# The group norm's inverse square root: one third-order step and one Newton step in place of three Newton steps

## The chip, the cores and the metric

The kernel runs on one core of a Trainium2 chip. The metric is the device time of one execution in microseconds (us). Three runs of the kernel before took 1077.81, 1078.03 and 1082.76 us, so the median is 1078.03 us. One more execution, the profiled one, is the source of every row below. The engines are called PE (TensorE matmuls), PEld (its weight loads), DVE (VectorE), ACT (ScalarE), POOL (GpSimd) and SP (SyncE, whose queue issues most transfers).

## What is computed

The reference is one step of a two-layer decoder trunk on 256 prompt tokens and 8 x 8 sample tokens (320 columns together). Layer 0 mixes tokens with a chunked gMLP, layer 1 with a Mamba-2 scan; each mixer is followed by a squared-ReLU MLP. All products are float32. The change touches the end of the Mamba-2 mixer, where the 2048 channels are cut into 8 groups of 256 and every group is divided by its own root mean square, for every token:

```python
y = y.reshape(bsz, l, D_INNER).astype(h.dtype) * jax.nn.silu(z)
yg = rms_norm(y.reshape(bsz, l, SSM_GROUPS, D_INNER // SSM_GROUPS), norm_g.reshape(SSM_GROUPS, -1))
out = yg.reshape(bsz, l, D_INNER) @ w_out
```

`rms_norm` multiplies with `rsqrt(mean(x * x) + EPS)`, where EPS is 1e-6, and with a gain.

## The kernel before, in words

**Layout.** Channels lie on the 128 partitions and the 320 tokens along the free dimension. Weights stream from HBM as tiles of 128 x 1024 (`raw`). `split` (line 133) makes two halves of each: ACT rounds it to `whi` (line 136), DVE subtracts to get `wlo` (line 137). `mm3` (line 305) then issues three matmuls of 320 columns per 128 x 128 block (lines 307 to 309), so that the sum has float32 precision.

**The Mamba stage.** Layer 1's mixer runs over the 8 groups `g_`. For each group, `convs` (line 804) projects six tiles (`in_tile`, 24 matmuls each), and `conv` (line 634) sums four shifted products on ACT and DVE (`co`, lines 646 and 649). `group_loads` (line 668) queues on SP the state and the two broadcast rows of decays (`bc`, line 673, and `ea`). `ssd` (line 677) is a generator, and the loop at line 865 advances the generator of the group before between the conv tiles of the current group, so two groups overlap. Its pieces in order: decay factors (lines 679 to 689, with `bc` computed by ACT at 687 and 688), transposes (693 to 729), state products (733 to 745), the output products (line 757) with `Y` on DVE (768) and POOL (769), then the group norm (773 to 780), then the state update (784 to 802).

**The group norm.** ACT squares `Y` (line 774) and DVE adds the two halves into `ta` (line 776). `mean_rstd` (line 222) lets PE take the mean over the partitions as three one-column products (`mean_mm`, line 210): token t of the block then sits on partition t, and the whole statistic is a tile of 128 x 3. On that tile DVE computes the negative inverse root: line 230 adds EPS, and `neg_rsqrt` (line 194) makes a first guess from the bits of the number (line 195) and refines it by three Newton steps of three instructions (lines 197 to 199). All of these stand in the trace with the tile name `nv`. `bcast` (line 201) then lets PE spread the result over the partitions (line 205: three matmuls with the negated identity `nid`, each of which leaves two records in the trace), and DVE scales `Y` into `yst` (line 780). `yst` is read only after the last group, by the output projection. Groups 0 to 6 go this way. Group 7 uses `root` (line 212) instead, with ACT's square root. `neg_rsqrt` is also called three times in layer 0, at line 537 (tile `mv`).

```python
        for _ in range(3):
            dve.tensor_tensor(a, r, r, MUL)
            dve.scalar_tensor_tensor(a, a, 0.5, v, MUL, MUL)
            dve.scalar_tensor_tensor(r, a, 1.5, r, SUB, MUL)
```

**The order of the work.** The program is written as data flow. A planner orders each engine's instructions at build time by walking through its own model of the times (line 1089, `schedule_with_timeline_sim=True`). On the chip, each engine executes its list in that fixed order. Two exceptions are written out by hand in this stage: `issue_after` at line 761 keeps the output products behind one of their own, and at line 796 the state update's. The statistic's matmuls and the broadcast share one PSUM buffer (pool `psn`, `nrm_ps`, line 110), so the mean of a group waits until line 780 of the group before has read the broadcast.

Of the kernel before, what the change touches and what calls it, by code (L numbers as in the profile page):

```python
# [9 lines left out]
I32 = mybir.dt.int32  # L10
AF = mybir.ActivationFunctionType
ALU = mybir.AluOpType
ADD, SUB, MUL, MIN, MAX = ALU.add, ALU.subtract, ALU.mult, ALU.min, ALU.max
# [18 lines left out]
EPS = 1e-6  # L32
# [20 lines left out]
def tile_trunk(ctx: ExitStack, tc: tile.TileContext, io):  # L53
    nc = tc.nc
    pe, act, dve, pool = nc.tensor, nc.scalar, nc.vector, nc.gpsimd
# [12 lines left out]
    def nm(s):  # L68
        uid[0] += 1
        return f"{s}{uid[0]}"  # L70
# [39 lines left out]
    def nrm_ps():  # L110
        return psn.tile([P, 512], F32, tag="nrm", name=nm("nrm"))
# [82 lines left out]
    def neg_rsqrt(r, v, a):  # L194
        dve.tensor_scalar(r.bitcast(I32), v.bitcast(I32), -0.5, 1597463007.0, MUL, ADD)
# [5 lines that stand above are left out]
    def bcast(r):  # L201
        pr = nrm_ps()
        for c in range(3):
            w = P if c < 2 else TS
            pe.matmul(pr[:, c * P : c * P + w], lhsT=r[:, c : c + 1].to_broadcast([P, P]), rhs=nid[:, P - w :], start=True, stop=True, skip_group_check=True)
        return pr[:, :T]

    def mean_mm(ps, q, ones, first, last):
        for c in range(3):
            pe.matmul(ps[:, c : c + 1], lhsT=q[:, OFFS[c] : OFFS[c] + P], rhs=ones[:, 0:1], start=first, stop=last, skip_group_check=True)  # L210

    def root(ps, t):
        s, v, r, a = (t[:, i, :3] for i in range(4))
        act.activation(s, ps[:, :3], AF.Sqrt, bias=eps)
        dve.tensor_scalar(v, ps[:, :3], EPS, None, ADD)
        dve.reciprocal(r, s)
# [3 lines that stand above are left out]
        return r  # L220

    def mean_rstd(q, ones, last=False):
        ps = nrm_ps()
        mean_mm(ps, q, ones, True, True)
        if last:
            t = tp.tile([P, 4, 4], F32, tag="nx", name=nm("nx"))
            return bcast(root(ps, t))
        s = tp.tile([P, 3, 4], F32, tag="nv", name=nm("nv"))
        v, r, a = s[:, 0, :3], s[:, 1, :3], s[:, 2, :3]
        dve.tensor_scalar(v, ps[:, :3], EPS, None, ADD)  # L230
        neg_rsqrt(r, v, a)
        return bcast(r)

    acc = {}
# [20 lines left out]
    def rstd_x(both=False):  # L255
        ps = acc["ps"]
        t = tp.tile([P, 4, 4], F32, tag="nx", name=nm("nx"))
        pr = bcast(root(ps, t))
        o = tp.tile([P, T], F32, tag="rstd", name=nm("rstd"))
        act.copy(o, pr)  # L260
        return (pr, o) if both else o
# [49 lines left out]
    def proj1(srcs, hi, lo, eng=dve):  # L311
        ps = mm_ps()
        n = 8 * len(srcs)
        for kc, src in enumerate(srcs):
            w = wload(src, eng=eng)
            for kk in range(8):
                k = kc * 8 + kk
                mm3(ps, w, kk, hi(k), lo(k), k == 0, k == n - 1)
        return ps
# [14 lines left out]
    def scaled(ps, r):  # L334
        c = tp.tile([P, 10], F32, tag="sc", name=nm("sc"))
        act.copy(c, ps[:, T:G])
        t = scratch()
        dve.tensor_tensor(t, ps[:, :T], r, MUL)
        dve.tensor_tensor(b1(t[:, TP:]), b1(t[:, TP:]), bb(c[:, 1:9]), ADD)
        dve.tensor_scalar(t[:, :TP], t[:, :TP], c[:, 0:1], None, ADD)  # L340
        return t
# [39 lines left out]
    for k in range(KD):  # L381
        sq = scratch()
        act.activation(sq, x[:, k, :], AF.Square)
        if k:
            a = tp.tile([P, T], F32, tag="acc", name=nm("acc"))
# [7 lines left out]
    v = gp.tile([P, 2, DG], F32, name="v")  # L393
# [188 lines left out]
    for m in range(KD):  # L582
        ps = proj1([io["gm_wo"][m, kc] for kc in range(2)], lambda k: uhi[:, k, :], lambda k: ulo[:, k, :])
# [36 lines left out]
    ps = scaled(pss[0], r0)  # L620
# [56 lines left out]
    def ssd(g_, st, bc, ea, B, C, X, Z):  # L677
# [97 lines left out]
        q1 = scratch()  # L775
        dve.tensor_tensor(q1, q0[:, 0], q0[:, 1], ADD)
        pr = mean_rstd(q1, ones_g, g_ == NG - 1)
        for r in range(2):
            m = 2 * g_ + r
# [180 lines left out]
    pr, r = rstd_x(True)  # L960
# [148 lines left out]
```

## Time and profile before

| what | value |
| --- | --- |
| median of three runs | 1078.03 us (1077.81 to 1082.76) |
| the profiled execution | 1075.66 us, span 1073.9 us |
| PE busy | 1030.2 us, 96% of the span |
| PEld busy | 970.8 us, 90% |
| DVE busy | 652.9 us, 61%, 1080 instructions |
| ACT busy | 549.2 us, 51% |
| POOL busy | 299.9 us, 28% |
| HBM | 199.31 MB read, 12.85 MB written |

The span runs from the first to the last instruction; the 1.76 us between it and the execution's time lie around it. Matmuls overlap in the trace, so a record's duration is longer than the step from its start to the next start. Where PE was idle, the timeline prints how long and what ended it. A DVE instruction's record, too, can overlap that of the next one.

### The profile page before, as it was taken

The numbers are of one execution on the slowest core, as the hardware profiler recorded it, in microseconds if no ns is written. First come the engines' busy times: TensorE is split into PE (matmuls) and PEld (weight loads), VectorE is DVE, ScalarE is ACT, GpSimd is POOL, SyncE is SP. The second block draws the span as 40 slices with busy tenths as digits, with TensorE's granted clock in tenths as the row PEclk, the third lists the DMA queues.
The fourth block names the chain that finished last, engine by engine and source line by source line (L and its number), as shares of the span: only waits on it lengthen the run. The fifth ranks groups of instructions, "written<-read, shape, count | busy, mean of one in ns | idle before, by whom it ended". The sixth has DMA issues, their size and how long they took to land.

```text
span 1073.9 us, 19747 instructions
## 1 busy us (share of the span) xinstructions
PE 1030.2 (96%) x7809; PEld 970.8 (90%) x7809; DVE 652.9 (61%) x1080; ACT 549.2 (51%) x1013; POOL 299.9 (28%) x403
## 2 busy tenths in 40 slices
PE   5999999999999999999688999999999999999996
PEld 3778998999999999999688999999999999999995
DVE  4545966437644443446968898898876754444432
ACT  4453343435644433335698777678345555543331
POOL 1200134332433311222123333532217243411001
PEclk9999999999999999999888999999999999999998
DMA  9957985775666667455435656565445544544431
GB/s 366 361 194 237 335 316 166 267 253 195 243 215 216 217 223 271 151 157 172 151 108 171 251 168 222 197 224 205 167 163 158 177 157 140 155 153 144 155 99 50
DMA packets 60877, 213.97 MB, mean 199 GB/s; under 512 B 6560, under 2 KB 12128, under 8 KB 58480
## 3 DMA queue, kind: packets, MB, share of 16 engines
q1 hardware_dynamic: 58544, 200.47, 55.1%
q0 software_dynamic: 1952, 11.98, 3.1%
q8 instruction: 61, 1.00, 0.4%
q10 hardware_dynamic: 288, 0.26, 0.1%
q14 instruction: 32, 0.26, 0.1%
HBM read 199.31 MB, written 12.85 MB: 198 GB/s over the span
## 4 chain that ended last, share of the span: by engine, by line
PE 76%; ACT 7%; DVE 6%; issue 5%; DMA 3%; POOL 2%; SPq 0%; POOLq 0%; ACTq 0%; DVEq 0%
PE mm L307 19%; PE mm L308 19%; PE mm L309 19%; PE adap L165 3%; ACT bc L687 2%; DMA bc<-rowd 2%; DVE wlo L137 2%; DVE co L649 2%; ACT whi L136 1%; PE mm L411 1%; PE mm L412 1%; PE mm L413 1%; PE ax L757 1%; DMA raw<-ada 1%; PE ax L307 1%
## 5 line engine op out<-in xcount | busy, mean ns | idle before, releaser
L137 DVE TENSOR_TENSOR wlo<-raw,whi 128x1024 fp32r<-128x1024 f32 (+1 forms) x243 | 298.1, 1228 | 203.5 <-ACT whi L136 202.6
L136 ACT ACTIVATE whi<-raw 128x1024 fp32r<-128x1024 f32 (+1 forms) x243 | 254.7, 1050 | 252.4 <-PE mm L308 195.0
L307 PE MATMUL mm<-hhi,whi 128*128 128x320 f32 x952 | 300.1, 316 | 1.9 <-ACT ta L356 0.9
L308 PE MATMUL mm<-hlo,whi 128*128 128x320 f32 x952 | 296.8, 313 | 0.1
L309 PE MATMUL mm<-hhi,wlo 128*128 128x320 f32 x952 | 296.9, 313 | 0.0
L307 PEld LDWEIGHTS mm<-hhi,whi 128*128 128x128 f32 x952 | 180.2, 190 | 7.5 <-issue 3.3
L308 PEld LDWEIGHTS mm<-hlo,whi 128*128 128x128 f32 x952 | 180.1, 189 | 1.9 <-DVE hlo L267 1.0
L309 PEld LDWEIGHTS mm<-hhi,wlo 128*128 128x128 f32 x952 | 180.0, 189 | 1.4 <-DVE mv L198 0.4
L307 PE MATMUL mm<-mhi,whi 128*128 128x320 f32 x512 | 158.3, 309 | 0.0
L308 PE MATMUL mm<-mlo,whi 128*128 128x320 f32 x512 | 158.1, 309 | 0.0
L309 PE MATMUL mm<-mhi,wlo 128*128 128x320 f32 x512 | 158.0, 309 | 0.0
L358 POOL TENSOR_TENSOR ta<-ta 128x320 f32<-128x320 f32 x64 | 82.0, 1285 | 140.0 <-ACT ta L356 118.2
L307 PEld LDWEIGHTS mm<-mhi,whi 128*128 128x128 f32 x512 | 96.1, 188 | 1.2 <-issue 0.8
L308 PEld LDWEIGHTS mm<-mlo,whi 128*128 128x128 f32 x512 | 96.1, 188 | 0.0
L309 PEld LDWEIGHTS mm<-mhi,wlo 128*128 128x128 f32 x512 | 96.1, 188 | 0.0
L293 POOL TENSOR_TENSOR x<-x,rs 128x64 f32<-128x64 f32 x28 | 11.2, 399 | 218.5 <-DVE rs L292 218.5
L359 ACT ACTIVATE mhi<-ta 128x320 fp32r<-128x320 f32 x64 | 30.1, 471 | 81.9 <-POOL ta L358 81.6
L360 DVE TENSOR_TENSOR mlo<-ta,mhi 128x320 fp32r<-128x320 f32 x64 | 33.5, 523 | 59.2 <-ACT mhi L359 59.2
L649 DVE SCALAR_TENSOR_TENSOR co<-cb,vec,co 128x344 f32<-128x344 f32 x96 | 54.7, 585 | 6.1 <-ACT co L646 5.9
L165 PE MATMUL adap<-ara,sc 128*32 128x256 f32 x640 | 43.0, 383 | 0.0
L307 PE MATMUL mm<-uhi,whi 128*128 128x320 f32 x128 | 40.0, 315 | 0.0
L308 PE MATMUL mm<-ulo,whi 128*128 128x320 f32 x128 | 40.0, 315 | 0.0
(340 smaller groups left out, 1691.8 us busy)
## 6 DMA issues: line engine op xcount, KB each, us to landing
raw<-mlp_w SPq DMA_DIRECT2D x128, 512.0 KB, 3.6
ara<-ada_w SPq DMA_DIRECT2D x80, 512.0 KB, 6.3
raw<-w_in SPq DMA_DIRECT2D x48, 512.0 KB, 3.7
raw<-ada SPq DMA_DIRECT2D x16, 512.0 KB, 9.9
raw<-gm_wv SPq DMA_DIRECT2D x16, 512.0 KB, 8.7
raw<-gm_wu SPq DMA_DIRECT2D x16, 512.0 KB, 5.8
raw<-gm_wo SPq DMA_DIRECT2D x16, 512.0 KB, 5.3
st<-state SPq DMA_DIRECT2D x8, 1024.0 KB, 5.5
```

The source lines that it names most:

```text
L136: act.activation(hi[:, :n], raw[:, :n], AF.Copy)
L137: eng.tensor_tensor(lo[:, :n], raw[:, :n], hi[:, :n].bitcast(F32), SUB)
L165: pe.matmul(ps[32 * j : 32 * j + 32, :256], lhsT=sc[:, kb + i, :], rhs=rs[i][:, j * 256 : (j + 1) * 256], start=(kb + i == AB - 1), stop=( ...
L293: (dve if m == KD - 1 else pool).tensor_tensor(x[:, m, TP:], x[:, m, TP:], t0, ADD)
L307: pe.matmul(ps[:, :n], lhsT=whi[:, kk, :], rhs=hi, start=first, stop=False)
L308: pe.matmul(ps[:, :n], lhsT=whi[:, kk, :], rhs=lo, start=False, stop=False)
L309: pe.matmul(ps[:, :n], lhsT=wlo[:, kk, :], rhs=hi, start=False, stop=last)
L358: pool.tensor_tensor(s, t, t, MUL)
L359: act.activation(mhi[:, m, :], s, AF.Copy)
L360: dve.tensor_tensor(mlo[:, m, :], s, mhi[:, m, :].bitcast(F32), SUB)
L649: dve.scalar_tensor_tensor(o[:, :CO], cb[:, k : k + CO], wv(k), o[:, :CO], MUL, ADD)
L687: act.activation(bc[:, h, cq[c]], bc[:, h, cq[c]], AF.Relu, bias=nat[:, c, HG * g_ + h : HG * g_ + h + 1], scale=-1.0)
```

## The change

It replaces the call of `neg_rsqrt` in `mean_rstd` by instructions of its own. `v` now holds 64/9 times the mean plus EPS, through the second operation of the instruction that adds EPS. The first guess from the bits is made as before, now from the scaled number. Then one step of third order follows (with x = r·r·v, r becomes r·(x·x − 10/3·x + 5), in four instructions; the factor 3/8 that such a step carries is taken up by the scaling) and one Newton step with the factor 9/64 folded into its constant (three instructions). The result is again the negative inverse root. Before, a call has 1 + 1 + 9 = 11 DVE instructions; after, 1 + 1 + 4 + 3 = 9. Tiles, buffers, matmuls and transfers are unchanged. Group 7 and layer 0 are not touched.

```diff
@@ -227,8 +227,15 @@
             return bcast(root(ps, t))
         s = tp.tile([P, 3, 4], F32, tag="nv", name=nm("nv"))
         v, r, a = s[:, 0, :3], s[:, 1, :3], s[:, 2, :3]
-        dve.tensor_scalar(v, ps[:, :3], EPS, None, ADD)
-        neg_rsqrt(r, v, a)
+        dve.tensor_scalar(v, ps[:, :3], EPS, 64.0 / 9.0, ADD, MUL)
+        dve.tensor_scalar(r.bitcast(I32), v.bitcast(I32), -0.5, 1597463007.0, MUL, ADD)
+        dve.tensor_tensor(a, r, r, MUL)
+        dve.tensor_tensor(a, a, v, MUL)
+        dve.scalar_tensor_tensor(a, a, -10.0 / 3.0, a, ADD, MUL)
+        dve.scalar_tensor_tensor(r, a, 5.0, r, ADD, MUL)
+        dve.tensor_tensor(a, r, r, MUL)
+        dve.scalar_tensor_tensor(a, a, 0.5 * 9.0 / 64.0, v, MUL, MUL)
+        dve.scalar_tensor_tensor(r, a, 1.5, r, SUB, MUL)
         return bcast(r)
```

## Rows read from the trace of the kernel before

**Rows 1.** The page: span, TensorE's line and its granted clock in 40 slices.
```profile
span 1073.9 us, 19747 instructions
...
PE   5999999999999999999688999999999999999996
...
PEclk9999999999999999999888999999999999999998
```

**Rows 2.** Seven stretches, one per group; each ends with clock, DMA share and GB/s.
```profile
core 0: us, PE busy (x) PEld busy (x) DVE busy (x) ACT busy (x) POOL busy (x), PEclk, DMA share, GB/s
...
615.00:645.00 30.00, 28.59 (x273) 27.66 (x274) 29.41 (x58) 22.28 (x49) 11.31 (x22) 1.00 0.53 174
...
737.00:768.00 31.00, 30.02 (x279) 28.54 (x278) 31.00 (x61) 20.84 (x47) 11.71 (x14) 1.00 0.42 146
...
sum 213.00, PE 209.13 PEld 199.69 DVE 188.11 ACT 141.50 POOL 76.45; mean PE 29.88 PEld 28.53 DVE 26.87 ACT 20.21 POOL 10.92
```

**Rows 3.** Tile nv: counts, ns min/median/max, first and last start; who waited for it.
```profile
L198 DVE SCALAR_TENSOR_TENSOR nv<-nv x21: 145/154/169, 591.9 to 774.3; 128x3 f32<-128x3 f32 x21
...
L230 DVE TENSOR_SCALAR nv<-nrm x7: 146/153/154, 587.3 to 768.2; 128x3 f32<-128x3 f32 x7
...
  DVE yst L780: 5.1, 1
```

**Rows 4.** TensorE's waits from 585 to 798 us: us in total, times, longest.
```profile
PE nrm L205 <- DVE nv L199: 2.0, 2, 1.3
PE adap L713 <- DVE Bst L704: 1.3, 2, 1.0
```

**Rows 5.** VectorE's timeline in group 0: start us, us, what.
```profile
586.80 0.57 DVE L649 SCALAR_TENSOR_TENSOR co<-cb,vec,co 128x344 f32<-128x344 f32 x1
587.29 0.15 DVE L230 TENSOR_SCALAR nv<-nrm 128x3 f32<-128x3 f32 x1
587.36 0.47 DVE L704 SCALAR_TENSOR_TENSOR Bst<-adap,cst,Bst 128x256 fp32r<-128x256 f32 x1
```

**Rows 6.** VectorE's timeline in group 6, at the end of its chain.
```profile
773.94 0.16 DVE L199 SCALAR_TENSOR_TENSOR nv<-nv 128x3 f32<-128x3 f32 x1
774.14 0.16 DVE L197 TENSOR_TENSOR nv<-nv 128x3 f32<-128x3 f32 x1
...
774.53 0.16 DVE L199 SCALAR_TENSOR_TENSOR nv<-nv 128x3 f32<-128x3 f32 x1
```

**Rows 7.** VectorE's and TensorE's timelines in group 1 around line 205.
```profile
626.95 0.15 DVE L197 TENSOR_TENSOR nv<-nv 128x3 f32<-128x3 f32 x1
...
627.66 0.16 DVE L199 SCALAR_TENSOR_TENSOR nv<-nv 128x3 f32<-128x3 f32 x1
...
627.88 0.88 PE L205 MATMUL nrm<-nid,nv 128*128 128x128 f32 x6 [1.30 <-DVE nv L199]
```

**Rows 8.** The same two timelines in group 4.
```profile
704.44 0.15 DVE L197 TENSOR_TENSOR nv<-nv 128x3 f32<-128x3 f32 x1
...
705.62 0.15 DVE L199 SCALAR_TENSOR_TENSOR nv<-nv 128x3 f32<-128x3 f32 x1
...
705.91 0.85 PE L205 MATMUL nrm<-nid,nv 128*128 128x128 f32 x6 [0.70 <-DVE nv L199]
```

**Rows 9.** The chain that ended last, 623 to 629 us: start us, us, what.
```profile
624.11 0.07 DVE nv L198
...
625.34 0.07 DVE nv L199
...
626.57 0.33 SPq L147
...
626.99 4.60 DMA bc<-rowd
```

**Rows 10.** VectorE's and TensorE's timelines in group 5 around line 205.
```profile
747.93 0.15 DVE L199 SCALAR_TENSOR_TENSOR nv<-nv 128x3 f32<-128x3 f32 x1
...
748.87 0.88 PE L205 MATMUL nrm<-nid,nv 128*128 128x128 f32 x6
```

## The prediction

> **What bounds the kernel now.** I read the page first. TensorE is busy for 1030.2 of 1073.9 us [rows 1], so whatever shortens the kernel must either take work from TensorE or remove one of its few idle moments. The change takes no matmul away. Its place comes from the rows of tile `nv`: the seven calls start between 587.3 and 768.2 us [rows 3], one per group of the Mamba stage. So the next view is that stage cut by groups. Over 213.0 us TensorE is busy for 209.13, which leaves 3.87 us idle, and VectorE is busy for 188.11, in single stretches almost throughout (29.41 of 30, 31.00 of 31) [rows 2]. The reader should see two things: TensorE sets the pace, but VectorE has little in hand, and it executes its list in order.
>
> The granted clock is below nine tenths only in the 20th to 22nd of 40 slices, 510 to 591 us [rows 1], and is 1.00 in the stretches shown [rows 2]. The planner walks forward in time, so the list up to the first changed instruction at 587.3 us should stay as it is, and those slices with it. I expect nothing from the clock.
>
> The third view is what TensorE waits for there. Its largest cause is the very chain that is shortened: line 205 waits for line 199 twice, 2.0 us together; the other large one, 1.3 us, is line 713 waiting for `Bst` [rows 4], which comes early in a group, before the refinement steps of the same group.
>
> **What the change removes, and its price.** Each call goes from 11 instructions to 9, all on tiles of 128 x 3, so 7 x 2 = 14 of VectorE's 1080 go. Those left are of the kinds already there; the multiplication by 64/9 rides on line 230 as a second operation. An instruction with two operations (line 198, 154 ns) takes as long as line 230 with one (153 ns) [rows 3], so I cost that edit at nothing. If a second operation did cost something, line 198's range (145 to 169 ns) bounds it by 24 ns, or 0.2 us for seven.
>
> The duration of a record isn't its price. In group 0 the record of line 230 lasts 0.15 us, but the next, independent instruction starts 0.07 us after it [rows 5]. That is the price where other work stands in between. In group 6 the last steps stand alone, each needing the one before, and start 0.20 us apart (773.94, 774.14) [rows 6]. So 14 instructions are worth between 14 x 0.07 = 1.0 us and 14 x 0.20 = 2.8 us of VectorE's time.
>
> The Trainium skill (VectorE: DVE Perf Modes, The DRAIN you can't avoid) says that the next vector operation does not start until the pipe of the last one has emptied. By that rule every removed record would give back its whole 0.154 us, 14 x 0.154 = 2.2 us. The trace disagrees for independent neighbours, where 0.07 us pass while the record still runs [rows 5], so the sum doesn't use it.
>
> How much of this is on the path that sets the end? There are two ways in.
>
> First, **TensorE's own waits on the chain**. In group 1 line 205 starts at 627.88 after 1.30 us of idle time, 0.22 us after the start of the ninth refinement instruction (627.66). The seventh started at 626.95, 0.71 us earlier [rows 7]. With seven steps and the same neighbours, the result is ready 0.71 us earlier. In group 4 the seventh starts at 704.44, the ninth at 705.62, 1.18 us later, and the wait is 0.70 [rows 8], so that wait would go. Together 0.71 + 0.70 = 1.4 us, if line 205 keeps its place among TensorE's instructions. It need not: the planner also sees a shorter chain and may put line 205 earlier by about as much, and the waits stay.
>
> Second, **VectorE's queue**. The chain that ended last passes through `nv` not for its result but for its slot: 0.07 us for line 198 and 0.07 for line 199, behind which VectorE's next split lets SP go on, and SP then issues the load of `bc`, which lands 4.60 us after 626.99 [rows 9]. Two slots fewer ahead of that pull SP's load forward by 0.14 us. If all seven groups have this, it is 7 x 0.14 = 1.0 us. No transfer is added, and none is moved past another by the edit itself.
>
> The two overlap, since both end in TensorE being sooner ready. What comes late next is the mean's product and `Bst`, which the edit doesn't touch. In group 6 nothing is gained: VectorE idles for 5.1 us until line 205 comes [rows 3], as the chain ended at 774.53 + 0.16, long before [rows 6]. I take 1.0 us, the value nearest to the slot that the chain of waits itself shows, with 0 and 2.8 us as ends.
>
> The profiled execution took 1075.66 us, 1.76 around its span of 1073.9, and lies 2.4 below the median of the runs, 1078.03. I take the sum off the median: 1078.03 − 1.0 = **1077.0 us**. What a measurement of this kernel can tell from no change is about 0.5%, or 5.4 us: faster means below 1072.6, slower above 1083.4.
>
> **The rivals.**
>
> *Nothing moves.* For it: five of seven groups don't wait on the chain at all; in the closest of them line 205 starts 0.79 us after the last step has ended (747.93 + 0.15 against 748.87) [rows 10]. Line 780's result is read only after the last group. If the planner also moves line 205 ahead by what the chain got shorter, the 2.0 us of waits stay as well. Against it: VectorE's stretches without any idle time [rows 2]. The time: 1078.0.
>
> The Trainium skill (Perfetto Trace Analysis, Identifying the Most-Contended Engine) says to improve the most contended engine first. On this rule, with TensorE at 209.13 of 213 us, the change gives nothing, as in this rival. The two waits on VectorE in rows 4 speak against it, and no row settles it.
>
> *The planner's new order removes other waits as well.* The list after the first changed instruction is planned anew, and the whole idle time of TensorE in the stage is 3.87 us [rows 2]. If all of it went, the time is 1078.0 − 3.9 = 1074.1. To pass 1072.6 it would have to gain outside the stage too, and there is no changed instruction there. For it speaks only that the order is planned; against it, that waits at line 713 hang on other work.
>
> *Line 205 comes too early.* This is the case on the slower side, and one mechanism. In TensorE's list line 205 is an instruction like any other, and while it waits all matmuls behind it wait. The planner places it by modelled times, in which the small steps may weigh more than on the chip; taking two away then moves line 205 further ahead than the real chain gets shorter. It decides from the point at which line 205 is moved by more than the reserve plus what the chain gains, 0.79 + 0.71 = 1.5 us in the closest group. Price: if all seven groups wait as long as the worst one now, 7 x 1.30 = 9.1 us in place of 2.0, so 1078.0 + 7.1 = 1085.1. For it: the two groups that already wait show that the plan runs ahead of the chip. Against it: five groups have a reserve, and the chain does get shorter on the chip.
>
> *The change doesn't do what it says.* That would be a chain that still has 11 instructions, or a result that needs another step. The diff has nine written out, so I give this no chance.
>
> **How the numbers follow.** Forecast (1075.2 to 1077.7): 0.52. Nothing moves: 0.24. New order better: 0.09, of which I put 0.06 below 1072.6, since a replanned list can change more than I can see here. Line 205 too early: 0.15, of which 0.13 lies beyond 1083.4. So faster 0.06, slower 0.13, same 0.81. The range leaves out at most 2 in 10. Its low end is the time without TensorE's idle time in the stage, 1074.1, less another 1.1 for the spread between the profiled execution and the runs. Its high end is 1083.2, where four of the seven groups (4 x 1.30 = 5.2) would newly wait.
>
> **What would show it right or wrong.** Right: tile `nv` shows 14 records fewer, 63 in place of 77; the slots between independent neighbours stay at about 0.07 us; TensorE's wait at line 205 for the chain falls from 2.0 us to about 0.6; its idle time in the stage goes from 3.87 to about 2.9 us; the clock outside slices 20 to 22 stays. Wrong: line 205 waits in more than two groups, or longer in total than 2.0 us (the third rival); the instructions before 587 us stand in another order, or the low-clock slices change, which I excluded; or TensorE gets a wait in the stage that is not in rows 4.

## The result, and the profile of the changed kernel

Seven runs of the changed kernel have a median of **1090.38 us** (1087.90 to 1096.23), seven of the kernel before on the same chip 1080.55 us (1077.5 to 1084.0). The ratio is **1.0104, interval 1.0080 to 1.0129**: the change costs 1%. In the experiment that ran the changed kernel once more it was 1.0110 [1.0083, 1.0136]. The forecast, 1077.0 us, and its range, up to 1083.2, both miss it. The profiled execution of the changed kernel took 1092.18 us, 1.8 around its span. Medians and ratios leave out slow executions, of which there was one (experiment 13: 1312.96 us at a mean granted clock of 0.731).

The page of the changed kernel, with the lines that answer to [rows 1]:

```profile
span 1090.4 us, 19730 instructions
...
PE 1037.7 (95%) x7809; PEld 976.5 (90%) x7809; DVE 653.8 (60%) x1066; ACT 549.2 (50%) x1013; POOL 302.1 (28%) x403
...
PE   5999999999999999999689999899899999999996
...
PEclk9999999999999999999899999899899999999998
```

VectorE has 14 instructions fewer (1066 for 1080), as the diff says. The busy shares are what they were. What is new stands in the last two lines: in the 26th and the 29th slice, 681 to 709 and 763 to 790 us, TensorE is less busy and its granted clock is lower. Before, both slices read 9.

In the changed kernel seven new lines stand behind line 231, so its line numbers are 7 higher from there: 774 is 781, 713 is 720, 307 is 314. Its tile `nv`, in the view that answers to [rows 3]:

```profile
L230 DVE TENSOR_SCALAR nv<-nrm x7: 149/155/161, 589.1 to 776.0; 128x3 f32<-128x3 f32 x7
...
L237 DVE SCALAR_TENSOR_TENSOR nv<-nv x7: 147/155/168, 597.4 to 789.4; 128x3 f32<-128x3 f32 x7
```

There are nine such lines with seven records each, 63 in place of 77. Line 230 now has two operations and takes 155 ns at the median, where it took 153 with one. What TensorE waited for from 585 to 798 us (us in total, times, longest), as in [rows 4]:

```profile
PE nrm L210 <- DVE ta L783: 4.9, 2, 4.0
PE mm L314 <- ACT Z L822: 2.9, 1, 2.9
PE mm L315 <- DVE hlo L881: 1.6, 1, 1.6
PE nrm L205 <- DVE nv L238: 1.1, 1, 1.1
```

The wait for the shortened chain (line 205) has indeed become shorter, 1.1 for 2.0 us. The first line has grown: the mean's product waits for VectorE's sum, which in the kernel before it did once, for 0.6 us. The two lines below it are new: two projection products wait for the gate `Z` and for `hlo`.

To compare stretches of the same work, I cut the stage at two marks: from the last output product (line 757, now 764) of group 1 to that of group 7. Of the kernel before, with the columns of [rows 2]:

```profile
596.30:782.50 186.20, 182.33 (x1705) 174.88 (x1701) 164.79 (x298) 128.08 (x280) 68.08 (x100) 1.00 0.57 199
```

Of the changed kernel, the same stretch, under it the stretches in it with the granted clock at 0.50, the lower of the two levels (1.2 of 2.4 GHz), and last a row of TensorE's timeline just ahead of it:

```profile
599.00:798.50 199.50, 189.24 (x1698) 181.42 (x1695) 165.65 (x284) 128.42 (x280) 70.52 (x100) 0.95 0.55 184
...
599.40:602.80 3.40, 3.40 (x17) 2.85 (x16) 3.40 (x4) 0.74 (x3) 2.45 (x1) 0.50 0.56 228
698.40:705.20 6.80, 4.32 (x17) 4.33 (x18) 4.30 (x8) 6.44 (x16) 0.58 (x1) 0.50 0.11 45
770.00:780.20 10.20, 9.42 (x38) 9.43 (x39) 6.72 (x14) 2.63 (x7) 0.58 (x1) 0.50 0.58 176
...
597.91 0.85 PE L205 MATMUL nrm<-nid,nv 128*128 128x128 f32 x6 [1.11 <-DVE nv L238]
```

The stage grew from 186.2 to 199.5 us, by 13.3 of the 16.5 us between the two spans. Of the rest, 0.5 us lie behind it and 2.7 ahead of it. The changed list already differs there: the broadcast of group 0 (line 205) has moved in between the last output products of group 1, and TensorE waits 1.11 us for it. But this mark also moves by more than that between executions with the same order ahead of it (596.3 us before, 605.3 in experiment 9).

TensorE's clock was at half for 3.4 + 6.8 + 10.2 = 20.4 us. Its busy time in the stage went from 182.33 to 189.24 us, and its idle time from 3.87 to 10.26. The products are the same but for the one broadcast that has moved ahead of the mark. So, as an estimate from these rows, about 6.9 of the 13.3 us go with the low clock and 6.4 are waits. Each low stretch lies at a wait: the first begins behind the 1.11 us that ended at 597.91, the other two within the waits shown next.

**Group 4.** The chain there runs from the output products over `Y` on VectorE, `Y` on POOL (line 769), ACT's square (774) and VectorE's sum (776) to the mean's product (210). The kernel before, timeline of ACT and TensorE (start us, us, what):

```profile
693.86 0.74 ACT L774 ACTIVATE Z<-Y 128x640 f32<-128x640 f32 x1 [5.55 <-POOL Y L769]
695.05 1.23 ACT L687 ACTIVATE bc<-bc,nat 128x128 f32<-128x128 f32 x4 [0.45 <-DMA bc<-rowd]
...
695.18 0.83 PE L210 MATMUL nrm<-ones_g,ta 128*128 128x1 f32 x6 [0.58 <-DVE ta L776]
```

The changed kernel, timelines of POOL, ACT and TensorE at the same place:

```profile
693.58 4.38 POOL L776 TENSOR_TENSOR Y<-Y,Z 128x640 f32<-128x640 f32 x1 [0.63 <-DVE Y L775]
...
698.74 0.93 ACT L694 ACTIVATE bc<-bc,nat 128x128 f32<-128x128 f32 x3 [5.13 <-DMA bc<-rowd]
699.58 0.72 ACT L781 ACTIVATE Z<-Y 128x640 f32<-128x640 f32 x1
...
700.88 1.44 PE L210 MATMUL nrm<-ones_g,ta 128*128 128x1 f32 x6 [4.04 <-DVE ta L783]
```

Before, ACT takes the square first and `bc` afterwards. In the changed kernel three `bc` activations stand ahead of the square. POOL is done at 697.96, but ACT sits until the load of `bc` lands at 698.74, and the square starts 1.6 us after POOL's end instead of at once. On TensorE's list the mean has also come forward: 30 projection matmuls lie between the group's output products and the mean instead of 43, and 13 x 0.147 us (their spacing at full clock) is 1.9 us. 0.58 + 1.6 + 1.9 = 4.1 us, against 4.04 in the trace.

**Group 6.** The changed kernel's POOL, ACT and TensorE:

```profile
761.55 6.42 POOL L776 TENSOR_TENSOR Y<-Y,Z 128x640 f32<-128x640 f32 x1 [3.85 <-DVE Y L775]
...
768.00 0.74 ACT L781 ACTIVATE Z<-Y 128x640 f32<-128x640 f32 x1 [6.35 <-POOL Y L776]
...
770.31 0.41 ACT L822 ACTIVATE Z<-mm 128x320 f32<-128x320 f32 x1
...
764.99 0.41 PE L315 MATMUL mm<-hlo,whi 128*128 128x320 f32 x1 [1.60 <-DVE hlo L881]
...
770.78 0.64 PE L314 MATMUL mm<-hhi,whi 128*128 128x320 f32 x1 [2.88 <-ACT Z L822]
```

Here the square has moved ahead of a weight split (line 136) and of the gate `Z`. ACT waits 6.35 us for POOL, the gate stands behind it, and the projection product waits 2.88 us for the gate. The 1.60 us for `hlo` lie earlier; experiment 4 will show that they don't hang on the square.

Neither place contains an instruction of the edit. Set side by side, the two kernels' lists agree up to the first changed instruction. Behind it, besides VectorE's own list, the planner has put 506 positions of TensorE's list in another order, 85 of ACT's, 19 of POOL's and 4 of SP's (two loads of `raw` change places with loads of the state).

### The profile page after: what moved, and what is told of

The parts are those of the page before. It is cut to its first block, busy times and chain, and to the rows that moved or that the text cites. A ratio compares the mean times of both kernels' runs of the same rounds, so it can differ in the third digit from the quotient of the medians.

```text
span 1090.4 us, 19730 instructions
## 1 busy us (share of the span) xinstructions
PE 1037.7 (95%) x7809; PEld 976.5 (90%) x7809; DVE 653.8 (60%) x1066; ACT 549.2 (50%) x1013; POOL 302.1 (28%) x403
## 4 chain that ended last, share of the span: by engine, by line
PE 75%; ACT 8%; DVE 6%; issue 5%; POOL 3%; DMA 3%; SPq 0%; POOLq 0%; ACTq 0%; DVEq 0%
PE mm L314 19%; PE mm L315 19%; PE mm L316 19%; PE adap L165 3%; ACT whi L136 2%; DMA bc<-rowd 2%; ACT bc L694 2%; DVE co L656 1%; DVE wlo L137 1%; POOL Y L776 1%; PE mm L418 1%; PE mm L419 1%; PE mm L420 1%; PE ax L764 1%; DMA raw<-ada 1%
## 5 line engine op out<-in xcount | busy, mean ns | idle before, releaser
L776 POOL TENSOR_TENSOR Y<-Y,Z 128x640 f32<-128x640 f32 x8 | 32.9, 4113 | 26.3 <-DVE Y L775 26.3
L694 ACT ACTIVATE bc<-bc,nat 128x128 f32<-128x128 f32 (+1 forms) x96 | 28.3, 375 | 23.5 <-DMA bc<-rowd 19.5
```

The lines of the kernel that those rows point to most:

```text
L694: act.activation(bc[:, h, cq[c]], bc[:, h, cq[c]], AF.Relu, bias=nat[:, c, HG * g_ + h : HG * g_ + h + 1], scale=-1.0)
L776: pool.tensor_tensor(Y, Y, Z, MUL)
```

## The experiments

From the trace I had a theory: **the arithmetic is worth nothing and the new order costs everything.** Rivals: the nine instructions themselves cost something, or one list alone (ACT's) carries the loss. To separate edit and order, experiments 1 to 9 and 12 to 14 write the lists out, as edges without any semaphore between neighbours on an engine, over the Mamba stage (in outline):

```diff
+    ORDER = {...}
+    for e_, places in ORDER.items():
+        for a_, b_ in zip(places, places[1:]):
+            tc.add_manual_dep(lists[e_][b_], lists[e_][a_].name, NoSync)
```

All the experiments' kernels keep the line numbers of the kernel before (all new steps stand in line 231). The kernel before, on the same chip as the runs that it is compared with, took 1079.46 us (experiments 1 to 4), 1079.25 (5 to 8), 1079.62 (9 to 12) and 1080.31 (13 to 15).

### Edit and order apart

Experiment 1 has the new nine instructions, and all lists as before, less the 14 instructions:

```diff
-        dve.tensor_scalar(v, ps[:, :3], EPS, None, ADD)
-        neg_rsqrt(r, v, a)
+        dve.tensor_scalar(v, ps[:, :3], EPS, 64.0 / 9.0, ADD, MUL)
...
+    ORDER = <the lists of the kernel before>
```

> The new arithmetic (9 instructions a call), with every engine's list held to the order of the kernel before; only the 14 removed instructions are missing from it. Theory (the time is lost by the new order of the lists, the arithmetic itself costs nothing): the ratio to the kernel before is 0.997 to 1.000, that is my forecast of 1.0 us less, and TensorE's waits for the chain at line 205 fall from 2.0 to about 0.6 us. Rival (the nine instructions themselves cost time on the chip): the ratio stays near 1.010.

Experiment 2 is the reverse, the old eleven instructions in the lists of the changed kernel:

```diff
+    ORDER = <the lists of the changed kernel>
```

> The old arithmetic (11 instructions a call), with every engine's list held to the order of the changed kernel; the two additional instructions stand directly behind the ninth. Theory (order alone): ratio 1.008 to 1.013, with stalls of TensorE of about 4 us near 697 us and 3 us near 768 us. Rival (arithmetic): ratio 1.000, no such stalls.

Experiment 1 took 1079.35 us, **1.0002** [0.9976, 1.0027]; experiment 2 took 1094.87 us, **1.0139** [1.0100, 1.0178]. The order carries the loss, and the arithmetic is worth nothing that could be measured. In the traces, the instructions of TensorE, VectorE, ACT and POOL follow one another in experiment 1 as in the kernel before, and in experiment 2 as in the changed kernel. Experiment 2's TensorE timeline has both large waits at the same work:

```profile
703.19 0.83 PE L210 MATMUL nrm<-ones_g,ta 128*128 128x1 f32 x6 [3.85 <-DVE ta L776]
...
773.26 0.63 PE L307 MATMUL mm<-hhi,whi 128*128 128x320 f32 x1 [2.88 <-ACT Z L815]
```

Experiment 1's waits of TensorE, 585 to 798 us, beside [rows 4], and where those at line 713 stand in its timeline:

```profile
PE adap L713 <- DVE Bst L704: 5.1, 3, 2.2
...
PE nrm L205 <- DVE nv L231: 0.6, 1, 0.6
...
616.90 0.44 PE L713 MATMUL adap<-cst,Xt 128*128 128x128 f32 x2 [2.02 <-DVE Bst L704]
...
709.56 0.44 PE L713 MATMUL adap<-cst,Xt 128*128 128x128 f32 x2 [0.95 <-DVE Bst L704]
...
741.85 0.44 PE L713 MATMUL adap<-cst,Xt 128*128 128x128 f32 x2 [2.18 <-DVE Bst L704]
```

The wait at line 205 went from 2.0 to 0.6 us, as forecast, but the waits at line 713 went from 1.3 to 5.1. The first of the three lies ahead of both places that waited at line 205, so it can't come from time saved there; it was 0.3 us before and is 0.33 in experiment 9, which has the same lists up to that point, so it differs between executions. The other two lie behind the wait of 0.70 us in group 4 that is gone [rows 8]: 0.95 us where there was none, and 2.18 for 1.0. There TensorE came sooner to a product whose operand wasn't ready, and the time saved at one wait was given back at the next. This is read from one execution of each kernel. The times alone don't show it: a gain of 1.0 us would also lie within the interval.

### Which part of the order

Experiments 3 and 4 start from the changed kernel and put instructions back. In 3 the square of group 4 goes ahead of the three `bc` activations; 4 also takes the square of group 6 behind split and gate again, with VectorE's sum behind it:

```diff
 ACT, group 4
-652 613 687 687 687 774 687
+652 613 774 687 687 687 687
 ACT, group 6 (experiment 4 alone)
-873 873 873 774 873 873 136 815
+873 873 873 873 873 136 815 774
```

> The changed kernel in its own order, except that ScalarE's square of group 4 (line 774 before) stands ahead of the three decay activations of group 6 that it stood behind, as in the kernel before. Theory A (ScalarE's list is what makes TensorE wait 4.0 us at the mean of group 4): the square starts when POOL's product ends, 1.6 us earlier, the wait falls to about 2.4 us, and with less low clock behind it the time falls by 1.6 to 5 us: ratio 1.005 to 1.009. Theory B (the mean's matmul stands too early in TensorE's own list, whatever ScalarE does): no gain beyond 1 us, ratio 1.009 to 1.013.

> As the run before, and in addition the square of group 6 and VectorE's sum behind it (line 776) stand behind the split and the gate that they stood in front of. Theory A: the 2.9 us wait of TensorE near 768 us (for the gate's evacuation, line 815 before) goes, and with it the low clock of 10.2 us from 770 us: a further 3 to 8 us, ratio 0.998 to 1.004. Theory B (other changes of the order matter as much): ratio above 1.006.

They took 1091.32 us (1.0096 [1.0066, 1.0125]) and 1086.84 us (1.0078 [1.0048, 1.0107]). One square alone brought nothing that can be told from the changed kernel, although the mean of group 4 then waited 2.5 us in place of 4.0, as the first reading had it. With both, the wait for `Z` is gone, but the one for `hlo` stays, and the mean's own place is still too early, now in group 6 as well (TensorE's waits in experiment 4):

```profile
PE nrm L210 <- DVE ta L776: 5.5, 3, 2.5
PE mm L308 <- DVE hlo L874: 1.6, 1, 1.6
```

Experiments 5 to 7 take the opposite way: the new arithmetic, all lists as before except one, which is the changed kernel's (TensorE's in 5, ACT's in 6, VectorE's in 7).

```diff
-    ORDER = <the lists of the kernel before>
+    ORDER = <the lists of the kernel before, but one engine's of the changed kernel>
```

> The new arithmetic; TensorE's list in the order of the changed kernel, all other lists in the order of the kernel before. Theory P (the planner put means and broadcasts too early into TensorE's list, and each wait there holds all matmuls behind it): waits at lines 205 and 210 of 1 to 3 us in groups 0, 3, 4, together 4 to 7 us, and ratio 1.004 to 1.009. Theory S (ScalarE's list holds the loss): ratio 0.998 to 1.003.

> The new arithmetic; ScalarE's list in the order of the changed kernel, all others as in the kernel before. Theory S: the square of group 4 waits behind decay activations whose rows have not landed, TensorE's wait at the mean of group 4 grows from 0.6 to about 2.2 us; the square of group 6 holds up the gate, 3 us at the matmul near 768 us; ratio 1.004 to 1.009. Theory P: ratio 0.998 to 1.003.

> The new arithmetic; VectorE's list in the order of the changed kernel, all others as before. Both theories: VectorE's list moves only the halves of yst for the output projection and the scaling of yst; ratio 0.998 to 1.004. Above 1.005 would say that VectorE's list carries the loss, which neither theory holds.

| new list | us | ratio | largest waits of TensorE |
| --- | --- | --- | --- |
| TensorE | 1089.58 | 1.0087 [1.0064, 1.0110] | mean (210) 5.8 us |
| ACT | 1090.72 | 1.0112 [1.0092, 1.0133] | gate `Z` (307) 4.1, mean 3.3, `Bst` (713) 2.4 |
| VectorE | 1091.57 | 1.0123 [1.0094, 1.0151] | mean 4.1, `hlo` (308) 2.4, `xe` (735) 2.0 |

Both readings fell: the parts don't add up to the whole. Each list alone costs about as much as all together, and no single engine's list is the culprit. The reading that fits, though it is not shown by itself: the chain around the mean passes through four engines with almost no reserve, and a list out of step with the others breaks it. POOL's and SP's new lists were not tried alone. In 6, ACT's new list meets the old loads, and ACT sits for 7.5 us ahead of the same `bc` activations (ACT's timeline):

```profile
701.97 0.93 ACT L687 ACTIVATE bc<-bc,nat 128x128 f32<-128x128 f32 x3 [7.50 <-DMA bc<-rowd]
```

### One instruction too early

Experiment 9 isolates the place that the slower rival should have had: experiment 1, with the mean of group 4 thirteen matmuls earlier and nothing else changed.

```diff
 TensorE, group 4
-<output products> <43 matmuls> 210 210 210
+<output products> <30 matmuls> 210 210 210 <13 matmuls>
```

> The run with the new steps in the old order, with one edit: the mean's matmuls of group 4 (line 210) stand 13 matmuls earlier in TensorE's list, where the changed kernel has them. Theory (a place without slack: product, POOL, square, sum and mean follow on one another through four lists, and TensorE's list decides when it looks for the last link): the wait at line 210 grows from about 0.5 to about 2.4 us, 13 matmuls at 0.147 us; with low clock behind it the ratio is 1.001 to 1.005. Rival (a wait there is taken back later, the stage is bound by VectorE anyway): wait as said, ratio 0.998 to 1.000.

The mean's record in experiment 1, then in experiment 9, there with its only wait at line 713:

```profile
696.85 0.83 PE L210 MATMUL nrm<-ones_g,ta 128*128 128x1 f32 x6 [0.52 <-DVE ta L776]
```

```profile
704.05 1.23 PE L210 MATMUL nrm<-ones_g,ta 128*128 128x1 f32 x5 [2.39 <-DVE ta L776]
...
624.12 0.44 PE L713 MATMUL adap<-cst,Xt 128*128 128x128 f32 x2 [0.33 <-DVE Bst L704]
```

The wait grew by 1.9 us, as 13 matmuls weigh, and 6.8 us at half clock began within it, at 703.4. But the time was 1080.49 us, 1.0009 [0.9993, 1.0025], an interval that reaches into both forecast ranges; the stage took 188.4 us, against 189.1 in experiment 1. The two waits at line 713 behind the moved mean (0.95 and 2.18 us) are gone, so there the operands had caught up, and at least part of what the wait cost was regained. The third (2.02 against 0.33) lies ahead of the move and has nothing to do with it. A single misplaced instruction is not the 1%.

### How large a part the clock has

Experiment 13 keeps the changed kernel's lists and puts 15 spare matmuls (128 x 320, into unused columns of the statistic's PSUM buffer) into the waits: seven ahead of the mean of group 4, three and five ahead of the two products in group 6. These do extra work that the output doesn't use. Experiment 14 repairs the two places instead: experiment 4, with the mean 13 matmuls later in group 4 and 17 in group 6. Experiment 15 is the changed kernel again, for comparison.

```diff
-        ps = nrm_ps()
+        ps = nrm_ps(); fc[0] += 1
+        for _ in range({5: 7, 7: 8}.get(fc[0], 0)):
+            pe.matmul(ps[:, 64 : 64 + T], lhsT=ident, rhs=mask, start=True, stop=True, skip_group_check=True)
```

> The changed kernel in its own order, with 15 additional matmuls (320 columns, float32, constants in, result read by nobody) at the three places where TensorE waits longest: seven ahead of the mean of group 4, three and five ahead of the two matmuls near 763 and 770 us. They fill the waits and shorten nothing. Theory C (the waits lower TensorE's clock, and the low clock is the larger part of the loss): the granted clock stays 1.00 from 690 to 790 us and the ratio is 1.001 to 1.006, though the same lists are in place. Theory W (the waits alone are the loss, the low clock comes by chance): ratio 1.008 to 1.014, and low clock as before.

> The changed kernel in its own order, with the two places set right in all lists: group 4's square ahead of the decays and its mean 13 matmuls later in TensorE's list; group 6's square behind the gate, its sum behind the split, and its mean 17 matmuls later. Theory (two places carry the loss): waits at line 210 fall under 1.5 us in both groups, no low clock there, ratio 0.998 to 1.004. Rival (many small shifts carry it): ratio 1.005 to 1.010.

> The changed kernel itself, on the same chip as the two runs before, for comparison. Ratio 1.008 to 1.013 by every theory; low clock near 698 and 770 us if it hangs on the waits.

The stage in experiment 13, and in it the mean of group 4 behind the spare matmuls:

```profile
599.90:792.10 192.20, 189.43 (x1726) 179.36 (x1724) 163.85 (x284) 128.35 (x280) 71.33 (x100) 1.00 0.55 189
...
697.07 3.93 PE L223 MATMUL nrm<-cst 128*128 128x320 f32 x14
...
701.30 0.83 PE L210 MATMUL nrm<-ones_g,ta 128*128 128x1 f32 x6 [0.29 <-DVE ta L776]
```

The stage in experiment 14, then in experiment 15:

```profile
599.70:791.30 191.60, 182.02 (x1698) 173.80 (x1694) 164.97 (x284) 128.35 (x280) 72.33 (x100) 1.00 0.56 190
...
598.00:795.40 197.40, 185.49 (x1696) 177.56 (x1692) 164.38 (x284) 128.33 (x280) 71.70 (x100) 0.97 0.55 186
```

| | us | ratio | stage, us | of it at half clock |
| --- | --- | --- | --- | --- |
| 13, waits filled | 1087.67 | 1.0078 [1.0058, 1.0098] | 192.2 | 0 |
| 14, two places repaired | 1086.26 | 1.0055 [1.0038, 1.0073] | 191.6 | 0 |
| 15, changed kernel | 1093.85 | 1.0110 [1.0083, 1.0136] | 197.4 | 10.2 |

With the waits filled, the mean is no sooner (701.30 against 700.88), but the low clock in the stage is gone, and the stage is 5.2 us shorter than in experiment 15, although TensorE does more. So the low clock comes from the waits and is not a thing of its own. The mean granted clock of the whole executions, profiled or not, fits this: 0.976 to 0.983 in the six of experiment 15, 0.983 to 0.985 in the five of experiment 13. What the clock alone costs can be estimated from experiments 14 and 15, which have the same products in the stage, 14 all at full clock: TensorE is busy for 182.02 and 185.49 us, so the 10.2 us at half clock cost 3.5 us, and the 20.4 us of the first profile 7.2. The rest of the loss is waiting. The whole time of experiment 13 improved by less than the stage: its ratio lies above the range forecast for the clock as the larger part (1.001 to 1.006), and its interval overlaps that of experiment 15.

The repair takes back about half of the loss, and its interval (up to 1.0073) lies below that of the changed kernel (from 1.0083). The ratio falls into the range of its rival, many small shifts. The other 0.55% is spread over waits of 0.8 to 2.1 us (lines 205, 735, 308, 713): TensorE is still idle for 9.6 us of the stage, against 3.9 before. Which of these waits it is stays open.

### The number of instructions

If the order is what counts, the time should not follow the number of instructions. Experiment 10 is the old arithmetic with one instruction more (12), experiment 11 the new one with one more (10), both with the planner's own lists; the added one computes r·r once more.

```diff
-        neg_rsqrt(r, v, a)
+        neg_rsqrt(r, v, a); dve.tensor_tensor(a, r, r, MUL)
```

> The old arithmetic with one instruction of its chain repeated at the end (its result is read by nobody), so 12 in place of 11 a call, and lists as the planner makes them. They agree with the kernel before up to group 6; there the mean stands 35 matmuls behind the output products in place of 67, and the square stands ahead of the gate's evacuation. Theory (places in the lists decide, and the number of instructions only through them): a stall of 2 to 4 us near 760 us, low clock behind it, ratio 1.003 to 1.009. Rival (fewer instructions disturb, more do not): ratio 0.998 to 1.002.

> The new arithmetic with one instruction of its chain repeated, 10 a call, lists as the planner makes them: they differ from both kernels; group 4's mean stands 43 matmuls behind the output products as in the kernel before, group 5's 30 in place of 64, and the squares of groups 1, 2 and 4 stand behind six decay activations. Theory (places): waits at the mean of group 5 of 2 to 4 us, ratio 1.004 to 1.013. Rival (the loss grows with the number of removed instructions): ratio 1.004 to 1.006, half of the change's.

| instructions in a call | us | ratio |
| --- | --- | --- |
| 9, the change | 1090.38 | 1.0104 [1.0080, 1.0129] |
| 10 | 1085.03 | 1.0055 [1.0039, 1.0071] |
| 11, before | 1080.55 | 1 |
| 12 | 1083.81 | 1.0033 [1.0016, 1.0050] |

Fewer is slower, and so is one more. The order of the kernel before is simply the best of the four that the planner drew. Taken alone, 10 instructions at half the loss of 9 would also fit a loss that grows with every instruction taken out; experiment 1 excludes that, with 9 instructions in the old order and no loss. In experiment 11 the mean of group 5 waits 2.8 us, as forecast from its place in the list. In experiment 10 the wait forecast at the mean of group 6 did not appear, though its ratio did.

### The waiting products moved back

Experiment 8 is experiment 1 with the waiting products moved back: line 713 fifteen matmuls later in groups 2, 4, 5 and 6, line 205 of group 1 six later, the mean of group 4 five later. Experiment 12 also moves line 735 ten matmuls later in three groups.

```diff
 TensorE, groups 2, 4, 5 and 6
-713 <15 matmuls>
+<15 matmuls> 713
```

> The new arithmetic in the old order, with TensorE's list alone edited where it waited: the transposes of line 713 stand 15 matmuls later in groups 2, 4, 5 and 6, the broadcast of group 1 six matmuls later, the mean of group 4 five later. If these waits cost what they show (5.1 us at line 713, 0.6 at line 205 and 0.5 at line 210 in the run with the old order), the ratio is 0.994 to 0.998 and TensorE's waits in the stage fall under 2 us. If the time is lost again at the next wait (VectorE, which reads line 713's output, then idles), the ratio is 0.999 to 1.002.

> As the run with the later transposes, and in addition the state products (line 735) of groups 2, 5 and 6 stand ten matmuls later, since TensorE waited there 3.1 us for VectorE. If TensorE's waits can be moved behind other matmuls once more: ratio 0.994 to 0.997. If VectorE's list is what bounds the stage by now: ratio 0.997 to 1.000, and the waits show up at another line.

Experiment 8 took 1078.11 us, 0.9979 [0.9960, 0.9997]. That is clearly better than the changed kernel, and better than the kernel before at the edge of what can be told. The waits were to fall under 2 us in total; they are 4.5, for the largest have moved on to the next product:

```profile
PE ax L735 <- DVE xe L725: 3.1, 3, 1.7
PE ax L735 <- ACT co L646: 0.8, 1, 0.8
PE nrm L210 <- DVE ta L776: 0.6, 1, 0.6
```

Experiment 12 took those away (1.6 us of waits are left, the stage is at full clock throughout and takes 184.3 us), yet the whole time is the same, 1077.66 us, 0.9990 [0.9977, 1.0002], which can't be told from the kernel before. The 2.4 us by which the stage is shorter than in experiment 8 (186.7) are less than what separates executions ahead of it.

## Why the prediction was wrong

**What held.** The records: 63 for 77. The second operation on line 230 costs no more than 2 ns at the median. The wait at line 205 falls to 0.6 us if the order stays (experiment 1), and so the 1.4 us of the first way was rightly sized for this wait. The lists before 587 us are unchanged.

**The step that failed** is the one that took the lists as fixed except for line 205: "the planner also sees a shorter chain and may put line 205 earlier by about as much", "no transfer is added, and none is moved past another by the edit itself". The prediction itself noted that everything behind the first changed instruction is planned anew. It drew from this that nothing ahead of it moves, and it allowed for a better order up to the whole idle time of the stage; but for a worse order it priced line 205 alone, with the waits already in [rows 4]. Experiments 1 and 2 show that this replanning is the whole effect: 1.0139 with the old arithmetic, 1.0002 with the new one in the old lists.

**"I expect nothing from the clock"** was the second failure, and it sized the range. [Rows 1] and [rows 2] show a stage at full clock, and experiment 13 shows that this hangs on its having no long waits; I took it for a property of the stage. Of the 13.3 us by which the stage grew in the profiled execution, some 7 are the clock's. No term of the sum and no rival contained it, so even seven waits at line 205 came to only 1085.1.

**The rival "Line 205 comes too early"** had the right side and kind: an instruction placed too early in a list that is executed in order. Its place was wrong. Line 205 waited less than before (1.1 us), and the waits were at the mean (210), at the gate and at `hlo`, ahead of the edit's own instructions on the group's chain. The reserve of 0.79 us that I read in [rows 10] belongs to an instruction that was not moved badly. The reserve that mattered, at the mean of group 4, was none at all: in the kernel before it already waited 0.58 us.

**The forecast gain of 1.0 us** is not shown, nor is it excluded, in the old order: experiment 1 gives 1.0002 [0.9976, 1.0027], and the gain would be 0.9991. In its trace the 1.4 us saved at line 205 stand against 2.1 us more at the two later waits of line 713 (0.95 + 2.18 − 1.0). "What comes late next is the mean's product and `Bst`" named this, but the sum didn't charge it. The Trainium skill (Perfetto Trace Analysis, Identifying the Most-Contended Engine) says to optimize the most contended engine first, which here is TensorE and not VectorE. Experiment 1, the edit alone, agrees (1.0002); the changed kernel shows that an order can lose 1% with the busy shares as they were.

**The slots.** The prediction set 0.07 us between independent neighbours against the Trainium skill (VectorE: DVE Perf Modes, The DRAIN you can't avoid). The same section also says that a next operation starts earlier when it is not held, that is, made to wait for all earlier ones. So [rows 5] need not contradict it; whether the neighbours there are held, no run shows.

**The signs** stated in advance did show it: waits that are not in [rows 4], and changed low-clock slices, were both named as what would make the prediction wrong.

## What to carry to other kernels

Where a planner orders the instructions, an edit of two small operations is a new draw of the whole order behind them: first compare the lists, then pin the old ones, and only then judge the edit by itself. Look in the profile for the chain with the least reserve across several engines (here products, VectorE, POOL, ACT, VectorE, mean), since any list that shifts on it costs a wait; and price a wait of TensorE of more than a microsecond with the half-clock stretch seen behind it, not by its length alone. A saving on a chain that TensorE waits for in one place is only worth something if the next operand is ready as well.

## What the runs showed of the hardware

- The granted clock fell to 0.50 at single waits of TensorE. In the changed kernel's profile it did so for 3.4 us behind one of 1.11 us, 6.8 us from within one of 4.04 us, and 10.2 us at 1.60 and 2.88 us close together; in experiment 9 for 6.8 us from within one of 2.39 us. Not every such wait did it, and not always for as long: experiment 15, with the same lists, has 1.09 us at the first place and no low clock there, and 3.4 us at the same 1.60 and 2.88 us; experiment 1 has a wait of 2.2 us and no low clock in the stage.
- POOL's product of 128 x 640 (line 769, in the changed kernel 776) has records of 3.55 us at the median of the changed kernel's eight, but 4.38 us in group 4 and 6.42 us in group 6, and ACT's square waits for all of it. The kernel before has long records at the same places, 4.41 and 6.02 us, so they are not of the change's making.
